# A grouped-query attention kernel: first K piece in two halves, early transposes moved behind score tiles, last period's order rewritten

## The chip, the cores and the metric

The kernel runs on one core of one Trainium2 chip. The metric is device time in microseconds (us), as a median of several executions; lower is better. The profile below is of one execution of the kernel before.

## The reference, cut to what matters

```python
batch, seq, n_heads, n_kv_heads, dim = 8, 512, 32, 8, 64      # float32 Q, K, V
K_expanded = np.repeat(K, 4, axis=2)                          # 4 heads of Q share one of K and V
V_expanded = np.repeat(V, 4, axis=2)
scores  = np.einsum('bhqd,bhkd->bhqk', Q, K_expanded) * scale # scale = 1/8, no mask
weights = np.exp(scores - scores.max(-1, keepdims=True))
weights = weights / (weights.sum(-1, keepdims=True) + 1e-10)
output  = np.einsum('bhqk,bhkd->bhqd', weights, V_expanded)
```

## The kernel before, in words

**Tiling.** Work is cut into 128 pairs of heads. For each pair the scores are made with the keys on the partitions, 128 keys at a time, so there are four score tiles of 128 x 1024 for a pair (512 queries of two heads side by side), and 512 in all. A score tile is two matmuls of 512 columns (line 241, in `scores`), which use the two halves of the array's rows beside each other. The exponential of a tile goes to ScalarE (ACT, line 255), or, for 78 of the 512 tiles, to a chain of steps on VectorE (DVE) and GpSimd (POOL) that builds the exponential out of bit patterns: `U` (line 266) and `F` (line 271) on DVE, `G` (line 276) and `W` (line 284) on POOL, and the join `P` (line 288) on DVE. The weighted sum with V (line 304, in `pv`) is 16 matmuls of 65 columns for each key chunk; the 65th column is the sum of the weights. `R` (line 320) takes the reciprocal of that sum and `N` (line 331) multiplies and writes the result; a store follows (line 372).

**Order.** The order of all this is written out by hand. `STEPS` (line 39) is the order of one period of 8 pairs, with 27 tiles on ACT and 5 on DVE and POOL, and 16 periods are run. `FINISH` (line 50) takes its place in the last one. A word of it is a step: `S9` fills the ninth score tile of ACT's list and `A9` is its exponential; `V1.6-8` is the last quarter of the weighted sum of pair 1; `D`, `U`, `F`, `G`, `W`, `P` with a number are the chain of that DVE tile; `T` and `C` transpose Q and copy it, `K` and `H` check V, `R` and `N` end a pair, `B` and `E` are small checks. `@1` names the period before, `a` and `b` the PSUM region. Each engine takes its own instructions strictly in that order: what stands behind a waiting instruction on TensorE (PE) waits too. There are two PSUM buffers for score tiles, so `S` of one tile waits until the exponential two tiles back is done.

**The opening.** Before the first period the kernel loads Q's first two heads (`q_start`, line 498) and K's first two heads (`k_start`, line 500) from the SP queue. K comes in two transfers: key chunk 0 (64 KB), then chunks 1 to 3 (192 KB). Further pieces come from the POOL queue (lines 505 to 516; `load_q` is line 149), with a few memsets in between. PE begins with eight idle matmuls of 512 columns on zeros (`spin`, line 493). DVE casts Q (line 522), ACT casts both K pieces (line 524), PE transposes Q (line 192 in `trans_q`) and K (line 171 in `first_k`), and DVE copies the transposes from PSUM (lines 195 and 173). PE's order is: spins, transposes of Q, transposes of K chunk 0, one more spin, transposes of K chunks 1 to 3, then score tiles. The transposes of what else the first two units need are listed in `EARLY` (line 214) by the number of the exponential behind which they are issued (line 437); all of them pass through the one buffer `d_ps`. Where the first period has no pair to sum yet, each `V` step of the order is replaced by as many idle matmuls of 256 columns as it has eighths (line 540).

The kernel ends with a flag: if a check fails, a general path runs instead (not run here).

Of the kernel before, what the change touches and what calls it, by code (L numbers as in the profile page):

```python
# [48 lines left out]
).split()  # L49
FINISH = (  # L50
# [10 lines left out]
).split()  # L61


# [19 lines left out]
def fast_path(ctx, tc, Q, K, V, out, flag):  # L83
    nc = tc.nc
    B, S, H, D = Q.shape
    KV = K.shape[2]
    HPG = H // KV
    SC = S // 128
# [38 lines left out]
    kn, qn, kt, qt = {}, {}, {}, {}  # L127

    def load_k(b, lo=0, hi=KV):
        if b not in kn:  # L130
            kn[b] = knat_pool.tile([128, SC, KV, D], BF16, name="k_nat")
        nc.gpsimd.dma_start(
            out=kn[b][:, :, lo:hi, :],
            in_=K[b, :, lo:hi, :].rearrange("(p sc) g d -> p sc g d", p=128),
        )
# [7 lines left out]
    def load_q(w, cuts=(0, 4 * HPG)):  # L143
        b, half = divmod(2 * w, GP)
        h0 = half * 2 * HPG
        if w not in qn:
            qn[w] = qnat_pool.tile([128, SC, 4 * HPG, D], BF16, name="q_nat")
        for lo, hi in zip(cuts[:-1], cuts[1:]):
            nc.gpsimd.dma_start(  # L149
                out=qn[w][:, :, lo:hi, :],  # L150
                in_=Q[b, :, h0 + lo:h0 + hi, :].rearrange("(sc p) h d -> p sc h d", p=128),
            )

    def d_tile():
        return d_pool.tile([128, 2, S], FP32, name="d_ps")
# [4 lines left out]
    def s_tile():  # L160
        return s_pool.tile([128, 2, S], FP32, name="s_ps")
# [4 lines left out]
    def first_k(gp, g, bank, lo=0, hi=SC):  # L166
        half_bank = bank.bitcast(BF16)[:, 0:S]
        ps = half_bank.rearrange("p (sc c) -> p sc c", sc=SC)
        for sc in range(lo, hi):
            for half in (0, 64):  # L170
                nc.tensor.transpose(ps[half:half + 64, sc, :], kn[0][:, sc, 2 * gp + g, :], ident)  # L171
        keys = slice(lo * 128, hi * 128)
        return lambda: nc.vector.tensor_copy(
            out=kt_first[:, gp, g, keys], in_=half_bank[:, keys]
        )
# [11 lines left out]
    def trans_q(u, g, bank, lo=0, hi=NPAIR):  # L187
        ps = bank.bitcast(BF16).rearrange("p (i sc c) -> p i sc c", i=NPAIR, sc=SC)
        for i in range(lo, hi):
            for sc in range(SC):  # L190
                h = ((u % 2) * 2 + g) * HPG + 2 * i
                nc.tensor.transpose(ps[:, i, sc, :], qn[u // 2][:, sc, h:h + 2, :], ident)  # L192
        if u not in qt:
            qt[u] = qt_pool.tile([128, 2, NPAIR, S], BF16, name="qt")
        return lambda: nc.vector.tensor_copy(  # L195
            out=qt[u][:, g, lo:hi, :], in_=ps[:, lo:hi, :, :].rearrange("p i sc c -> p i (sc c)")
        )
# [10 lines left out]
    def early_q(g, lo):  # L208
        return lambda bank: trans_q(0, g, bank, lo)

    def early_k(gp, g):
        return lambda bank: first_k(gp, g, bank)

    EARLY = {1: [early_q(0, 1)], 2: [early_k(0, 1)], 3: [early_q(1, 0)], 5: [early_k(1, 0)],
             6: [early_k(1, 1)]}

    every = [(p, kc) for p in range(PPAIR) for kc in range(SC)]
    ON_DVE = [(p, kc) for p, kc in every if kc in DVE_KCS[p]]
# [30 lines left out]
    def fill(p, kc):  # L249
        ps = s_tile()  # L250
        scores(p, kc, ps)
        filled[p, kc] = ps
# [166 lines left out]
    def step(tok, n):  # L419
        what, k = tok[0], int(tok[1:].split(".")[0].rstrip("ab"))  # L420
        q, kc = ON_DVE[k] if what in "DUFGWPgwsa" else (0, 0)
        if what == "S":
            fill(n * PPAIR + ON_ACT[k][0], ON_ACT[k][1])
            if k == 9 and n == 0:
                dma_k(0, TURNED)
            if k == 2 and n % 2 == 1 and n // 2 + 1 < B:
                dma_k(n // 2 + 1)
        elif what == "A":
            q, kc = ON_ACT[k]
            p = n * PPAIR + q  # L430
            exp_act(p, kc)
            if ON_ACT[k + 1:k + 2] == [] or ON_ACT[k + 1][0] != q:
                for d, (dq, dkc) in enumerate(ON_DVE):
                    if dq == q and not on_dve(n, d):
                        fill(p, dkc)
                        exp_act(p, dkc)
            if n == 0 and k in EARLY:
                bank = d_tile()
                for copy in [turn(bank[:, 1, :]) for turn in EARLY[k]]:
                    copy()  # L440
            if (n, k) == (0, 4):
                second_loads()
        elif what in "VRN":
            p = n * PPAIR + k
            if what == "V":
                lo, hi = tok[3:].rstrip("abs").split("-")
                pv(p, int(lo), int(hi), tok)
            else:
                (inverse if what == "R" else norm)(p)
        elif what in "TKCH":  # L450
            j = n * PPAIR // NPAIR + k
            if j < 2:
                pass
            elif what == "T":
                transposes(j, region(tok))
            elif what == "K":
                check_values(j)
            else:
                read(j if what == "C" else (j, "v"))
        elif what == "Q":  # L460
            loads(n, k)
        elif what == "B":
            if n < NPER - 1:
                bulk_check(n)
        elif what == "E":
            (early_check, verdict)[k]()
        elif what in "sa":
            (fill if what == "s" else exp_act)(n * PPAIR + q, kc)
        elif on_dve(n, k):
            p = n * PPAIR + q  # L470
            if what == "D":
                exp_fill(p, kc, region(tok))
                return
            st = chain.get((p, kc))
            if what == "U":
                exp_bits(st)
            elif what == "F":
                exp_low(st)
            elif what in "Gg":
                slope(nc.gpsimd if what == "G" else nc.vector, st["f"], st["g"])  # L480
            elif what in "Ww":
                bend(nc.gpsimd if what == "W" else nc.vector, st["f"], st["g"], st["w"])
            elif what == "P":
                exp_join(p, kc)
# [9 lines left out]
                bank[:, 1, 0:columns], warm[:, 0:128], warm[:, 0:columns], start=True, stop=True  # L494
            )

    START = ((0, 1), (1, SC))
    nc.sync.dma_start(out=q_start, in_=Q[0, :, 0:2, :].rearrange("(sc p) h d -> p sc h d", p=128))  # L498
    for raw, (lo, hi) in zip(k_start, START):
        nc.sync.dma_start(  # L500
            out=raw[:, lo:hi, :, :],
            in_=K[0, :, 0:2, :].rearrange("(p sc) g d -> p sc g d", p=128)[:, lo:hi, :, :],
        )
    make_identity(nc, ident)
    load_q(0, (2, 4, 8))
    nc.gpsimd.memset(ones, 1.0)
    nc.gpsimd.memset(off, 0)
    for j in range(2):
        for c in (0, VW - 1):
            nc.gpsimd.memset(vt[j][:, :, :, c:c + 1], 1.0)  # L510
    load_k(0, 2, 4)
    load_q(0, (8, 16))
    load_v(0, 0, 1)
# [6 lines left out]
    nc.scalar.activation(out=early, in_=warm[:, 0:1], func=EXP, scale=scale)  # L520
    spin(8, S)
    nc.vector.tensor_copy(out=qn[0][:, :, 0:2, :], in_=q_start)
    for raw, (lo, hi) in zip(k_start, START):
        nc.scalar.copy(out=kn[0][:, lo:hi, 0:2, :], in_=raw[:, lo:hi, :, :])  # L524
    copies = [trans_q(0, 0, s_tile()[:, 0, :], 0, 1), first_k(0, 0, d_tile()[:, 0, :], 0, 1)]
    for copy in copies:
        copy()
    spin(1, S)
    copy = first_k(0, 0, s_tile()[:, 0, :], 1, SC)
    copy()  # L530

    for period in range(-2, NPER):
        for entry in STEPS if period < NPER - 1 else FINISH:
            tok, _, late = entry.partition("@")
            n = period - int(late or 0)
            if 0 <= n < NPER:
                step(tok, n)
            elif period == 0 and n < 0 and tok[0] == "V":
                lo, hi = tok[3:].rstrip("abs").split("-")
                spin(int(hi) - int(lo), S // 2)  # L540


def general_path(tc, Q, K, V, out):
# [114 lines left out]
```

## Time and profile before

| | |
|---|---|
| median of 3 runs | 415.19 us (413.82 to 415.45) |
| the profiled execution | 415.06 us, of which the span of the profile is 413.2 us |
| ACT busy | 400.7 us (97% of the span) |
| PE busy | 380.7 us (92%) |
| DVE busy | 334.3 us (81%) |
| POOL busy | 276.6 us (67%) |

All times in the profile are counted from the start of the span; 1.9 us of the profiled execution lie outside it. A row of the timeline has the start, the duration from the first start to the last end, the engine, the line, the operation, what it writes and reads with sizes, and the count; in brackets stands how long the engine was idle before it and who ended that. On ACT and PE the instructions overlap: one exponential alone takes 1.02 to 1.06 us while the next one starts about 0.92 us after it.

### The profile page before, as it was taken

The page shows a single profiled execution, that of the slowest core. Times are in us where ns is not written, and L with a number is a line of the kernel's source. Part 1 is how long each engine was busy: PE and PEld are TensorE (multiplying, and loading weights), DVE is VectorE, ACT ScalarE, POOL GpSimd, SP SyncE. Part 2 cuts the span into 40 slices and gives each one's busy share as a digit, 9 for nine tenths or more (in the row PEclk, how much of TensorE's full clock was granted, in tenths as well). Part 3 has the DMA queues.
Part 4 walks back from the last instruction along what each step waited for, and adds up shares of the span by engine and source line. Part 5 has one row for each costly group of instructions (what it writes and reads, how often), then busy time and mean ns, then how long its engine had stood idle before and what let it go on. Part 6 is the DMA issues. An engine that isn't in the chain of part 4 may idle for free.

```text
span 413.2 us, 13322 instructions
## 1 busy us (share of the span) xinstructions
PE 380.7 (92%) x5825; PEld 242.1 (59%) x5825; DVE 334.3 (81%) x617; ACT 400.7 (97%) x438; POOL 276.6 (67%) x208
## 2 busy tenths in 40 slices
PE   8999989899998999989899998999989899998995
PEld 3556656566565655656565565656656565665553
DVE  2488897878889788897878889788797878889885
ACT  4999999999999999999999999999999999999994
POOL 8066776677766677676676766667776677766750
PEclk9999999999999999999999999999999999999998
DMA  9969788687769797589865979849788698652205
GB/s 148 197 123 191 190 157 200 156 165 175 158 169 179 129 215 176 138 192 238 170 122 136 181 168 216 202 105 172 194 158 198 165 167 173 158 161 103 103 37 174
DMA packets 65406, 67.74 MB, mean 164 GB/s; under 512 B 35264, under 2 KB 39872, under 8 KB 65344
## 3 DMA queue, kind: packets, MB, share of 16 engines
q0 software_dynamic: 28128, 24.91, 41.1%
q1 hardware_dynamic: 37216, 41.95, 34.4%
q8 instruction: 46, 0.75, 0.7%
q14 instruction: 16, 0.13, 0.1%
HBM read 50.33 MB, written 33.55 MB: 203 GB/s over the span
## 4 chain that ended last, share of the span: by engine, by line
ACT 76%; PE 20%; DMA 1%; DVE 1%; issue 1%; SPq 0%; ACTq 0%
ACT pt L255 76%; PE s_ps L241 9%; PE pv L304 5%; PE d_ps L304 3%; DMA k_start<-in_K_dram 1%; PE pv L493 1%; PE d_ps L192 1%; DVE pt L288 0%; PE d_ps L171 0%; ACTq L255 0%; DVE o_sb L331 0%; PE s_ps L171 0%; ACT k_nat L524 0%; SPq L500 0%; SPq L498 0%
## 5 line engine op out<-in xcount | busy, mean ns | idle before, releaser
L255 ACT ACTIVATE pt<-s_ps 128x1024 f16<-128x1024 f32 x434 | 398.4, 1283 | 2.8 <-PE s_ps L241 2.8
L304 PEld LDWEIGHTS <-pt 128*128 128x128 f16 x4096 | 142.4, 98 | 65.9 <-issue 55.0
L241 PE MATMUL s_ps<-qt,kt 64*128 64x512 bf16 x810 | 158.8, 383 | 23.1 <-ACT pt L255 20.0
L284 POOL TENSOR_TENSOR w<-g,f 128x1024 bf16<-128x1024 bf16 x77 | 164.1, 2132 | 6.4
L276 POOL TENSOR_SCALAR g<-f 128x1024 bf16<-128x1024 int16 x77 | 80.5, 1045 | 115.7 <-DVE f L271 115.7
L304 PE MATMUL pv<-v,pt 128*128 128x65 bf16 x2560 | 114.8, 195 | 0.2
L241 PEld LDWEIGHTS <-kt 64*128 64x128 bf16 x960 | 57.0, 93 | 65.2 <-issue 34.9
L266 DVE TENSOR_SCALAR u<-d_ps 128x1024 int16<-128x1024 f32 x48 | 58.6, 1221 | 19.8 <-PE d_ps L241 19.8
L304 PE MATMUL d_ps<-v,pt 128*128 128x65 bf16 x1536 | 66.6, 194 | 1.2 <-DVE pt L288 0.9
L331 DVE TENSOR_TENSOR o_sb<-pv,inv 128x512 f32<-128x512 f32 x80 | 55.3, 692 | 2.8
L288 DVE TENSOR_TENSOR pt<-u,w 128x1024 uint16<-128x1024 int16 x78 | 54.3, 698 | 2.1 <-POOL w L284 1.1
L192 PEld LDWEIGHTS <-q_nat 128*128 128x128 bf16 x512 | 29.4, 98 | 14.7 <-issue 10.9
L266 DVE TENSOR_SCALAR u<-pv 128x1024 int16<-128x1024 f32 x30 | 36.5, 1216 | 0.0
L195 DVE COPY qt<-d_ps 128x1024 bf16<-128x1024 bf16 (+1 forms) x48 | 32.7, 680 | 3.4 <-PE d_ps L192 3.4
L331 DVE TENSOR_TENSOR o_sb<-d_ps,inv 128x512 f32<-128x512 f32 x48 | 33.2, 691 | 1.6
L271 DVE TENSOR_SCALAR f<-u 128x1024 int16<-128x1024 int16 x78 | 32.7, 419 | 0.1
L192 PE MATMUL d_ps<-ident,q_nat 128*128 128x128 bf16 x380 | 29.8, 222 | 0.0
L320 DVE RECIPROCAL inv<-pv 128x8 f32<-128x8 f32 x80 | 16.5, 206 | 10.5 <-PE pv L304 7.5
L320 DVE RECIPROCAL inv<-d_ps 128x8 f32<-128x8 f32 x48 | 10.0, 208 | 15.6 <-PE d_ps L304 15.1
L241 PE MATMUL d_ps<-qt,kt 64*128 64x512 bf16 x90 | 17.5, 375 | 0.0
L204 DVE TENSOR_REDUCE okv<-d_ps 128x1 f32<-128x128 f32 x31 | 8.9, 287 | 9.3 <-PE d_ps L203 9.3
L149 POOL DMA_DIRECT2D q_nat<-in_Q_dram x18 | 14.7, 815 | 0.2 <-issue 0.2
(49 smaller groups left out, 116.6 us busy)
## 6 DMA issues: line engine op xcount, KB each, us to landing
out_dram<-o_sb SPq DMA_DIRECT2D x31, 1024.0 KB, 5.8
q_nat<-in_Q_dram POOLq DMA_DIRECT2D x15, 1024.0 KB, 9.1
k_nat<-in_K_dram POOLq DMA_DIRECT2D x7, 512.0 KB, 5.2
kt<-kt SPq DMA_DIRECT2D x14, 256.0 KB, 4.4
v<-in_V_dram POOLq DMA_DIRECT2D x7, 512.0 KB, 7.8
out_dram<-o_sb SPq DMA_DIRECT2D x4, 256.0 KB, 2.5
q_nat<-in_Q_dram POOLq DMA_DIRECT2D x1, 512.0 KB, 7.1
v<-in_V_dram POOLq DMA_DIRECT2D x4, 128.0 KB, 7.8
```

Of the source, the lines that this page charges most:

```text
L192: nc.tensor.transpose(ps[:, i, sc, :], qn[u // 2][:, sc, h:h + 2, :], ident)
L195: return lambda: nc.vector.tensor_copy(out=qt[u][:, g, lo:hi, :], in_=ps[:, lo:hi, :, :].rearrange("p i sc c -> p i (sc c)"))
L241: nc.tensor.matmul(ps[:, m, :], keys[64 * m:64 * m + 64, g if early else g ^ m, kc * 128:(kc + 1) * 128], qt[u][64 * m:64 * m + 64, g, i, ...
L255: nc.scalar.activation(out=pt_of(p)[:, kc, :, :], in_=filled.pop((p, kc)), func=EXP, scale=scale)
L266: nc.vector.tensor_scalar(out=st["u"], in0=st["ps"], scalar1=A_U, scalar2=B_U, op0=ALU.mult, op1=ALU.add)
L271: nc.vector.tensor_single_scalar(out=st["f"], in_=st["u"], scalar=1023, op=ALU.bitwise_and)
L276: engine.tensor_scalar(out=g, in0=f, scalar1=-EXP_F1, scalar2=EXP_K * 2.0 ** (24 * (engine is nc.gpsimd)), op0=ALU.add, op1=ALU.mult,)
L284: engine.tensor_tensor(out=w, in0=g, in1=f, op=ALU.mult)
L288: nc.vector.tensor_tensor(out=pt_of(p)[:, kc, :, :].bitcast(U16), in0=st["u"], in1=st["w"], op=ALU.add)
L304: nc.tensor.matmul(sums[p][:, m, qc, :], pt_of(p)[:, kc, m, qc * 128:(qc + 1) * 128], vt[b % 2][:, kc, gp, g * (D + 1):(g + 1) * (D + 1)], ...
L320: nc.vector.reciprocal(out=invs[n][:, k], in_=sums[p][:, :, :, s:s + 1])
L331: nc.vector.tensor_tensor(out=osb[u][:, :, h:h + 2, :].rearrange("p qc m d -> p m qc d"), in0=sums.pop(p)[:, :, :, o:o + D], in1=invs[p // ...
```

## The change

Four things, in the diff's order from the bottom up:

1. K's first piece is loaded in two halves of two key chunks each (128 KB and 128 KB). ACT casts the first half, DVE the second. PE transposes the first half, fills the first score tile, and then transposes the second half. The single spin between the pieces goes.
2. The early transposes are issued right behind the score tile `S` of their number instead of behind the exponential `A` of that number. One of them (the first of Q's second group) moves from number 3 to number 4, and number 0 is new: it is the second half of K.
3. On POOL the first two loads of Q's further heads are issued behind the memsets instead of ahead of them. The idle matmuls in the first period have 128 columns instead of 256.
4. `FINISH` is written anew: same steps, another order. The other 15 periods keep `STEPS`.

```diff
 FINISH = (
-    "F1 V5.1-2@1 C1 V5.2-3@1 G1 S1 V5.3-4@1 H1 V5.4-6@1 A0 S2 P4@1 V7.0-1a@1 V5.6-7@1 "
-    "V7.1-2@1 V5.7-8@1 V7.2-3@1 A1 W1 V7.3-4@1 R5@1 S3 N5@1 V7.4-6@1 A2 S4 V6.0-2b@1 "
-    "V7.6-8@1 A3 V6.2-3@1 R7@1 S5 F0 V6.3-5@1 N7@1 V6.5-6@1 G0 A4 S6 V6.6-8@1 D2a A5 R6@1 S7 "
-    "W0 N6@1 U2 A6 S8 T2b A7 S9 C2 V1.0-4a F2 A8 S10 P0 V0.0-2b V1.4-6 P1 A9 S11 V0.2-3 G2 "
-    "V0.3-4 V1.6-8 A10 S12 R1 V0.4-5 N1 V0.5-7 W2 V0.7-8 A11 S13 R0 D3a N0 A12 S14 U3 "
...
-    "V6.7-8 V7.1-2 A25 V7.2-3 R6 V7.3-5 N6 V7.5-6 A26 V7.6-8 R7 N7 E1 "
+    "F0 P4@1 S1 V5.1-3@1 H1 G0 V5.3-4@1 C1 A0 S2 V5.4-8@1 W0 A1 S3 R5@1 V7.0-1a@1 N5@1 "
+    "V7.1-4@1 A2 S4 V6.0-4b@1 A3 V7.4-5@1 F1 S5 P0 V6.4-7@1 A4 V6.7-8@1 S6 G1 R6@1 V7.5-6@1 "
+    "N6@1 V7.6-8@1 A5 S7 R7@1 T2b W1 N7@1 A6 S8 C2 D2a U2 A7 S9 V0.0-5b A8 S10 F2 V0.5-8 G2 "
+    "A9 S11 R0 V1.0-1a N0 V1.1-4 A10 W2 S12 D3b V1.4-6 A11 S13 A12 P1 A13 U3 V1.6-8 S14 R1 "
...
+    "R6 V7.2-4 N6 V7.4-6 B0@2 A26 V7.6-8 R7 N7 E1 "
 ).split()
...
-    EARLY = {1: [early_q(0, 1)], 2: [early_k(0, 1)], 3: [early_q(1, 0)], 5: [early_k(1, 0)],
-             6: [early_k(1, 1)]}
+    EARLY = {0: [early_k(0, 0, SC // 2)], 1: [early_q(0, 1)], 2: [early_k(0, 1)],
+             4: [early_q(1, 0)], 5: [early_k(1, 0)], 6: [early_k(1, 1)]}
...
         if what == "S":
             fill(n * PPAIR + ON_ACT[k][0], ON_ACT[k][1])
+            if n == 0 and k in EARLY:
+                bank = d_tile()
+                for copy in [turn(bank[:, 1, :]) for turn in EARLY[k]]:
+                    copy()
...
-            if n == 0 and k in EARLY:
-                bank = d_tile()
-                for copy in [turn(bank[:, 1, :]) for turn in EARLY[k]]:
-                    copy()
...
-    START = ((0, 1), (1, SC))
+    START = ((0, SC // 2), (SC // 2, SC))
...
     make_identity(nc, ident)
-    load_q(0, (2, 4, 8))
     nc.gpsimd.memset(ones, 1.0)
...
+    load_q(0, (2, 4, 8))
     load_k(0, 2, 4)
...
-    for raw, (lo, hi) in zip(k_start, START):
-        nc.scalar.copy(out=kn[0][:, lo:hi, 0:2, :], in_=raw[:, lo:hi, :, :])
-    copies = [trans_q(0, 0, s_tile()[:, 0, :], 0, 1), first_k(0, 0, d_tile()[:, 0, :], 0, 1)]
-    for copy in copies:
+    (lo, mid), (mid, hi) = START
+    nc.scalar.copy(out=kn[0][:, lo:mid, 0:2, :], in_=k_start[0][:, lo:mid, :, :])
+    for copy in [
+        trans_q(0, 0, s_tile()[:, 0, :], 0, 1), first_k(0, 0, d_tile()[:, 0, :], lo, mid)
+    ]:
         copy()
-    spin(1, S)
-    copy = first_k(0, 0, s_tile()[:, 0, :], 1, SC)
-    copy()
+    nc.vector.tensor_copy(out=kn[0][:, mid:hi, 0:2, :], in_=k_start[1][:, mid:hi, :, :])
...
-                spin(int(hi) - int(lo), S // 2)
+                spin(int(hi) - int(lo), S // 4)
```

More of the change, by code (lines that the diff above doesn't have):

```diff
@@ L209, in early_q, with early_k @@
         return lambda bank: trans_q(0, g, bank, lo)
-    def early_k(gp, g):
-        return lambda bank: first_k(gp, g, bank)
-    EARLY = {1: [early_q(0, 1)], 2: [early_k(0, 1)], 3: [early_q(1, 0)], 5: [early_k(1, 0)],
-             6: [early_k(1, 1)]}
+    def early_k(gp, g, lo=0):
+        return lambda bank: first_k(gp, g, bank, lo)
+    EARLY = {0: [early_k(0, 0, SC // 2)], 1: [early_q(0, 1)], 2: [early_k(0, 1)],
+             4: [early_q(1, 0)], 5: [early_k(1, 0)], 6: [early_k(1, 1)]}
     every = [(p, kc) for p in range(PPAIR) for kc in range(SC)]
```

8 rows, old and new, of the table FINISH are left out of this document.

## The prediction, as it was made

> **What bounds the kernel now.** I read the page first, then the chain of waits from end to end, then the timeline of the first 17 us and of the last 30.
>
> ```profile
> span 413.2 us, 13322 instructions
> PE 380.7 (92%) x5825; PEld 242.1 (59%) x5825; DVE 334.3 (81%) x617; ACT 400.7 (97%) x438; POOL 276.6 (67%) x208
> L255 ACT ACTIVATE pt<-s_ps 128x1024 f16<-128x1024 f32 x434 | 398.4, 1283 | 2.8 <-PE s_ps L241 2.8
> L276 POOL TENSOR_SCALAR g<-f 128x1024 bf16<-128x1024 int16 x77 | 80.5, 1045 | 115.7 <-DVE f L271 115.7
> L288 DVE TENSOR_TENSOR pt<-u,w 128x1024 uint16<-128x1024 int16 x78 | 54.3, 698 | 2.1 <-POOL w L284 1.1
> ```
>
> ScalarE is the bound: 434 exponentials fill 97% of the span and it is idle only 2.8 us among them. The change alters neither their number nor their size, so it can only move the first one, close gaps between them, or shorten what follows the last.
>
> ```profile
> 17.19 11.11 ACT pt L255 x12
> 78.28 6.86 ACT pt L255 x8
> 127.78 6.86 ACT pt L255 x8
> 391.03 2.05 DVE pt L288 x2
> 407.87 0.43 PE d_ps L304 x8
> 409.03 0.60 DVE o_sb L331
> ```
>
> The chain (start, length) repeats itself in the middle. The same place comes at 78.28 and two periods of 27 exponentials later at 127.78, so the steady pace is 49.50/54 = 0.917 us. That is the yardstick for both ends. The middle periods keep their order, and I cost them at nothing.
>
> **The opening now.** Its rows of the timeline:
>
> ```profile
> 3.73 0.30 ACT L524 CAST k_nat<-k_start 128x128 bf16<-128x128 f32 x1 [1.35 <-DMA k_start<-in_K_dram]
> 5.28 0.32 PE L171 MATMUL d_ps<-ident,k_nat 128*64 128x128 bf16 x2
> 5.39 0.42 DVE L195 COPY qt<-s_ps 128x512 bf16<-128x512 bf16 x1 [1.27 <-PE s_ps L192]
> 5.73 0.21 DVE L173 COPY kt_first<-d_ps 128x128 bf16<-128x128 bf16 x1
> 6.07 0.51 ACT L524 CAST k_nat<-k_start 128x384 bf16<-128x384 f32 x1 [2.04 <-DMA k_start<-in_K_dram]
> 6.63 0.53 PE L171 MATMUL s_ps<-ident,k_nat 128*64 128x128 bf16 x6 [0.49 <-ACT k_nat L524]
> 7.10 1.13 PE L241 MATMUL s_ps<-qt,kt_first 64*128 64x512 bf16 x4
> 7.21 0.36 DVE L173 COPY kt_first<-s_ps 128x384 bf16<-128x384 bf16 x1 [1.26 <-PE s_ps L171]
> 7.62 0.10 PEld L241 LDWEIGHTS <-kt_first 64*128 64x128 bf16 x2 [0.42 <-DVE kt_first L173]
> 7.75 1.94 ACT L255 ACTIVATE pt<-s_ps 128x1024 f16<-128x1024 f32 x2 [1.17 <-PE s_ps L241]
> 8.16 0.61 PE L493 MATMUL pv<-warm 128*128 128x256 bf16 x2
> 8.56 0.64 PE L192 MATMUL d_ps<-ident,q_nat 128*128 128x128 bf16 x4
> 8.99 0.64 PE L493 MATMUL pv<-warm 128*128 128x256 bf16 x2
> 9.56 0.61 PE L241 MATMUL s_ps<-qt,kt_first 64*128 64x512 bf16 x2
> 10.21 2.87 ACT L255 ACTIVATE pt<-s_ps 128x1024 f16<-128x1024 f32 x3 [0.52 <-PE s_ps L241]
> 10.64 0.39 PE L241 MATMUL s_ps<-qt,kt_first 64*128 64x512 bf16 x2
> 12.18 0.61 PE L192 MATMUL d_ps<-ident,q_nat 128*128 128x128 bf16 x8
> 12.83 0.69 DVE L195 COPY qt<-d_ps 128x1024 bf16<-128x1024 bf16 x1 [0.99 <-PE d_ps L192]
> ```
>
> Both operands of the first score tile are in SBUF at 5.94 (5.73 + 0.21). It starts at 7.10 because PE is in order and stands at 6.63 waiting for the large K piece. From 7.75 to 17.19 nine exponentials start; at 0.917 they would take 8.25, so 1.19 us are lost on top of the late start. PE is slow here: a tile takes 0.61 at 9.56 and 0.39 at 10.64. Until about 10.6 a tile holds PE for 0.54 before the idle matmuls that follow (7.62 to 8.16), a transpose of 128 columns for 0.107 (four from 8.56 to 8.99), and a change of matmul shape costs about 0.11 (included in the 0.54).
>
> **The change there, step by step.** *First tile.* K's first 64 KB were in at 3.73 and all 256 KB at 6.05; in proportion to bytes the new 128 KB half lands at 4.50. Its cast of 256 columns lies between 0.30 and 0.51; I take 0.40, so 4.90, which is before PE is through with Q at 5.28. Its four transposes (between the 0.32 of two and the 0.53 of six) take 0.42. The copy to SBUF starts at 5.73 as now and takes 0.28 (between 0.21 and 0.36): 6.02. The tile starts 0.05 later, as at 7.62, needs 0.61, and ACT begins 0.04 after its end: 6.07 + 0.61 + 0.04 = 6.72, **1.03 before** 7.75.
>
> *Second half.* It lands by 6.05, the same bytes in all. DVE is free then and casts it in about 0.33 (ACT's rows give 0.30 to 0.51): 6.38. PE reaches its transposes at 6.07 + 0.54 = 6.61 and the second tile at 6.97; that tile ends at 7.58, and the second exponential is due at 6.72 + 0.92 = 7.64. The new wait is covered, by 0.06 only: a half that comes 0.5 later costs about 0.3.
>
> *Tiles 3 and 4.* Behind tile 2 now stand four Q transposes and then four spins at 0.107: 6.97 + 0.54 + 0.43 + 0.43 + 0.13 for the change of shape = 8.50, done 9.11, exponential at 9.15; due 7.64 + 0.92 = 8.56, lost 0.59. Behind it eight K transposes side by side in twos (0.43), two spins (0.21) and two changes of shape: 8.50 + 0.54 + 0.43 + 0.21 + 0.22 = 9.90, exponential at 10.55; due 10.07, lost 0.48. Tile 5 starts at 9.90 + 0.54 + 0.21 + 0.11 = 10.76, now fast, and is in time.
>
> *Later.* The eight Q transposes go from behind exponential 3 to behind tile 4. At about 12.6 their 0.69 copy starts, and the K transposes behind the next tile wait for the one buffer; the tile queued behind those comes about 0.24 late. Losses are 0.59 + 0.48 + 0.24 = 1.31 against 1.19 now. **The opening gives 1.03 - 0.12 = 0.91 us.** From the rows it may be 0.2 (halves 0.5 to 1 us later than by bytes) to 1.9 (PE fast from 8.5, so that 0.59 and 0.48 go).
>
> *POOL.* Two loads go behind the memsets:
>
> ```profile
> 1.61 1.71 POOL L149 DMA_DIRECT2D q_nat<-in_Q_dram  x2 [0.16 <-issue]
> 3.31 0.12 POOL L506 MEMSET ones<- 128x1 bf16 x1
> 3.43 0.40 POOL L510 MEMSET v<- 128x16 bf16 x4
> q_nat<-in_Q_dram POOLq DMA_DIRECT2D x1, 128.0 KB, 4.7
> ```
>
> The memsets take about 0.5 (3.31 to 3.83), so this piece lands at 1.61 + 0.5 + 4.7 = 6.8 instead of 6.3. PE wants it at 6.97 + 0.54 = 7.51: hidden, by 0.7. The loads behind keep their places. K's halves share the DMA engines with it for half a microsecond less, which is worth nothing to a few tenths; I take nothing.
>
> **The last period.**
>
> ```profile
> 379.05 14.08 ACT L255 ACTIVATE pt<-s_ps 128x1024 f16<-128x1024 f32 x15
> 390.95 2.13 DVE L288 TENSOR_TENSOR pt<-u,w 128x1024 uint16<-128x1024 int16 x2
> 391.12 1.41 POOL L276 TENSOR_SCALAR g<-f 128x1024 bf16<-128x1024 int16 x1 [1.30 <-DVE f L271]
> 393.13 0.41 PE L304 MATMUL d_ps<-v,pt 128*128 128x65 bf16 x8 [0.87 <-DVE pt L288]
> 393.91 13.91 ACT L255 ACTIVATE pt<-s_ps 128x1024 f16<-128x1024 f32 x15 [0.78 <-PE s_ps L241]
> ```
>
> Fifteen starts lie between 379.05 and 393.91: 14.86 us, 1.11 more than 15 x 0.917. The last fifteen run at pace (14 x 0.917 + 1.06 = 13.90). The stall is one place: `P0 P1` stand together on DVE beside POOL's G2, all three slow (2.13 for two instead of 2 x 0.70, 1.41 instead of 1.05), `V1.6-8` waits for P1, and `S12` is queued behind it.
>
> In the new order P0 comes after `F1`, five score tiles before `V0.5-8`. P1 follows `N0`: after pair 0's sum come R0, N0 and P1, some 0.2 + 0.7 + 0.7 us, while three score tiles (2.75) are placed between `V0.5-8` and `V1.6-8`, whose matmuls and those of V1 fill PE. So P1 has about half a microsecond in hand beyond what PE needs; the 0.37 that a join grew by here fits in. The rest of the order spreads the joins in the same way. I take 1.0 of the 1.11 back; nothing if a new pile-up is as bad, and up to 1.5 if the small gaps of the steady pace go too.
>
> *Tail.* After the last exponential come the same eight matmuls (407.87), the same DVE steps to 409.63 and the same store; `B0@2` moves ahead of it, where DVE waits anyway. Nothing, within 0.2.
>
> **Sum:** 0.91 + 1.0 = 1.9, made against the profiled execution's 415.06: **413.1**. That execution stands 0.1 below the median of 415.19.
>
> **Rivals.**
>
> *PE is fast sooner, or the last period runs smoother than the middle.* Without the 0.59 and 0.48 the opening gives 1.0 more: 412.0. For it: PE idles less after 6.1 than now. Against it: nothing in the trace sets the moment.
>
> *PE is fast later.* The idle matmuls that kept it busy are halved, and one of 512 columns goes. If it stays slow to about 14, the eight Q transposes (0.86) with three spins and the tile make a slot of 1.8 instead of 0.92; with the slot before, 0.16 + 0.91 - 0.24 = 0.83 is lost: 413.9.
>
> *Slower than before: PE stays slow far into the weighted sums.* From 17 on a slot needs a tile (0.54) and 16 matmuls of 65 columns at 0.054 (half the 0.107): 1.41 instead of 0.92, a loss of 0.35 per us. The gain of 1.9 is gone at 14 + (1.9 - 0.83)/0.35 = 17, and at 24 the kernel stands at 417.4. Against it: once these sums begin PE has no gap left. The Trainium skill, "TensorE: Matmul & The Clock Gate", says in Part 1 that the clock is released by a busy window of some 3.4 us at a phase that the kernel doesn't set, and in Part 4 that transposes don't count as busy. By that rule the two last rivals gain, since in the new opening transposes take the place of idle matmuls between 7.5 and 10.6; the fast row at 10.64 after four transposes in the stretch neither confirms nor excludes it.
>
> *It doesn't do what it says.* The last period stalls again at another join, or a K half lands a microsecond late: one of the two gains falls away, 414.1.
>
> **How the numbers follow.** About 0.5% (2.1 us) is what a measurement of this kernel can tell from no change. Forecast 0.62, with its own range 412.4 to 413.8, a little more than half of it beyond the bound: 0.34 faster, 0.28 same. PE sooner or a smoother end 0.14, faster. PE later 0.08, same. One gain missing 0.08, same. Slower 0.08. Together 0.48, 0.44, 0.08. The range 411.8 to 414.8 leaves out the slow rival and the ends of the others.
>
> **What would show it.** The first exponential starts at about 6.7 and the second without a gap; PE transposes K's second half between the first two tiles. The tenth exponential starts about 0.9 before 17.19. No exponential of the last period waits 0.5 us for PE, and no join is waited for by PE. The prediction is wrong if tiles still take 0.61 after 11 us, if DVE's cast of the second half ends after 6.6, or if the middle periods change their pace.

## The result, and the profile after

The changed kernel takes 411.90 us (median of 6 runs, 411.44 to 412.04). The kernel before took 414.98 beside it (6 runs, 413.82 to 415.45). The ratio is 0.993, with a 95% interval of 0.9915 to 0.9945: faster by 3.1 us, where the forecast was 1.9 (413.1, with a range of 411.8 to 414.8).

The profiled execution took 411.91 us, 3.15 less than the one profiled before. Its page:

```profile
span 410.1 us, 13319 instructions
PE 377.7 (92%) x5824; PEld 242.2 (59%) x5824; DVE 334.1 (81%) x618; ACT 399.9 (98%) x437; POOL 276.6 (67%) x208
L254 ACT ACTIVATE pt<-s_ps 128x1024 f16<-128x1024 f32 x434 | 398.0, 1292 | 2.2 <-PE s_ps L240 2.2
```

The lines have moved up by one (254 was 255, 240 was 241, 303 was 304). The same 434 exponentials are there, and ScalarE's wait for score tiles is 2.2 us in place of 2.8; all 2.2 now lie ahead of the first exponential. The timeline of the opening of the changed kernel:

```profile
4.03 0.40 ACT L523 CAST k_nat<-k_start 128x256 bf16<-128x256 f32 x1 [1.65 <-DMA k_start<-in_K_dram]
4.72 0.63 PE L191 MATMUL s_ps<-ident,q_nat 128*128 128x128 bf16 x4
5.29 0.42 PE L170 MATMUL d_ps<-ident,k_nat 128*64 128x128 bf16 x4
...
6.10 0.45 PE L240 MATMUL s_ps<-qt,kt_first 64*128 64x512 bf16 x2 [0.40 <-DVE kt_first L172]
6.49 0.30 PE L170 MATMUL d_ps<-ident,k_nat 128*64 128x128 bf16 x4
6.60 13.98 ACT L254 ACTIVATE pt<-s_ps 128x1024 f16<-128x1024 f32 x15 [2.16 <-PE s_ps L240]
6.72 0.39 PE L240 MATMUL s_ps<-qt,kt_first 64*128 64x512 bf16 x2
...
8.64 0.39 PE L240 MATMUL s_ps<-qt,kt_first 64*128 64x512 bf16 x2
```

PE fills the first tile (6.10), transposes K's second half (6.49) and fills the second tile (6.72), as laid out. The exponentials run from 6.60 on as one row of 15. And a score tile takes 0.39 from the second one on; before, a tile still took 0.61 at 9.56. PE has its full clock some 4 us sooner (6.27 instead of 10.67). No term of the forecast's sum had that; one of its rivals did.

The last period of the changed kernel, and the end of its chain of waits:

```profile
373.11 31.55 ACT L254 ACTIVATE pt<-s_ps 128x1024 f16<-128x1024 f32 x34
379.71 0.68 DVE L287 TENSOR_TENSOR pt<-u,w 128x1024 uint16<-128x1024 int16 x1
...
390.10 0.75 DVE L287 TENSOR_TENSOR pt<-u,w 128x1024 uint16<-128x1024 int16 x1
```

```profile
404.72 0.43 PE pv L303 x8
...
405.88 0.60 DVE o_sb L330
```

Thirty-four exponentials in a row, with no idle time before any; the last one alone is 1.24 long, so the 33 starts before it took 30.31, against 33 x 0.917 = 30.26. The joins shown (0.68 and 0.75) stand alone, where two took 2.13 before, and the other four of this stretch take 0.68 or 0.69.

**Where the 3.15 came from**, by the starts of the exponentials in the two traces:

| | before | after | gain |
|---|---|---|---|
| first exponential | 7.75 | 6.60 | 1.15 |
| from there to the tenth | 9.44 (at 17.19) | 8.37 (at 14.97) | 1.07 |
| to the last but one ahead of the last period's `A0` | 362.77 | 362.68 | 0.09 |
| the 28 starts after that one | 26.81 | 25.77 | 1.04 |
| from the last start to the end of the span | 6.45 | 6.64 | -0.19 |

The last 28 starts are the one ahead of `A0` and the 27 of the last period. Counted from `A0` itself, its 26 further starts take 25.00 before and 23.89 after: 1.11, and the middle gives 0.01.

### The profile page after: what moved, and what is told of

Same layout as the page of the kernel before. It is cut to its first block, busy times and chain, and to the rows that moved or that the text cites. A ratio compares the mean times of both kernels' runs of the same rounds, so it can differ in the third digit from the quotient of the medians.

```text
span 410.1 us, 13319 instructions
## 1 busy us (share of the span) xinstructions
PE 377.7 (92%) x5824; PEld 242.2 (59%) x5824; DVE 334.1 (81%) x618; ACT 399.9 (98%) x437; POOL 276.6 (67%) x208
## 4 chain that ended last, share of the span: by engine, by line
ACT 77%; PE 20%; issue 1%; DVE 1%; ACTq 0%
ACT pt L254 77%; PE s_ps L240 9%; PE pv L303 6%; PE d_ps L303 4%; PE pv L492 1%; PE d_ps L191 0%; DVE qt L194 0%; ACTq L254 0%; DVE o_sb L330 0%; PE s_ps L191 0%; PE d_ps L170 0%; PE d_ps L202 0%; DVE warm L517 0%; DVE kt_first L172 0%; DVE off L343 0%
## 5 line engine op out<-in xcount | busy, mean ns | idle before, releaser
L265 DVE TENSOR_SCALAR u<-d_ps 128x1024 int16<-128x1024 f32 x47 | 57.4, 1221 | 19.9 <-PE d_ps L240 19.9
L287 DVE TENSOR_TENSOR pt<-u,w 128x1024 uint16<-128x1024 int16 x78 | 53.4, 685 | 2.2 <-POOL w L283 0.8
L265 DVE TENSOR_SCALAR u<-pv 128x1024 int16<-128x1024 f32 x31 | 37.7, 1216 | 0.0
```

The lines of the kernel that those rows point to most:

```text
L265: nc.vector.tensor_scalar(out=st["u"], in0=st["ps"], scalar1=A_U, scalar2=B_U, op0=ALU.mult, op1=ALU.add)
L287: nc.vector.tensor_tensor(out=pt_of(p)[:, kc, :, :].bitcast(U16), in0=st["u"], in1=st["w"], op=ALU.add)
```

## The experiments

**The theories.** Two things were to be told apart. *The order theory:* the opening gains by its order alone (halves, tiles that start sooner, fewer idle matmuls), and PE's full clock at 6 in one profile was chance. *The clock theory:* a good part of the opening's gain is PE's clock; the new order leaves PE no long idle stretch at 6 us, and so the clock opens sooner in most executions. For the last period, the theory was that P1's lateness behind P0 makes the stall, and the rival that the stall is spread over the whole old order. The kernels were measured in three groups, each with its own runs of the kernel before (21, 17 and 10 of them); each ratio is to those.

**1. The opening alone** (`e1_open`): the changed kernel with the old order of the last period.

```diff
 FINISH = (
-    "F0 P4@1 S1 V5.1-3@1 H1 G0 V5.3-4@1 C1 A0 S2 V5.4-8@1 W0 A1 S3 R5@1 V7.0-1a@1 N5@1 "
...
+    "F1 V5.1-2@1 C1 V5.2-3@1 G1 S1 V5.3-4@1 H1 V5.4-6@1 A0 S2 P4@1 V7.0-1a@1 V5.6-7@1 "
...
```

> The changed kernel with the last period's order of before: only the opening is changed. If the opening brings the 0.91 us of the prediction and about 1.1 more because its own work makes PE fast sooner (tiles of 0.39 from the second on), the time is 2.0 to 2.2 us under before, near 412.8, in every run. If the early fast PE was a chance of the executions measured, the runs spread as those of before do (1.6 us), with a median about 0.9 under before, near 414.0.

Measured: 412.86 (10 runs, nine of them 412.62 to 413.09, one 414.24), ratio 0.9957 (0.994 to 0.9974). The stall of the last period is there again; in the timeline of this kernel:

```profile
388.64 2.12 DVE L288 TENSOR_TENSOR pt<-u,w 128x1024 uint16<-128x1024 int16 x2
...
391.60 13.91 ACT L255 ACTIVATE pt<-s_ps 128x1024 f16<-128x1024 f32 x15 [0.78 <-PE s_ps L241]
```

So the opening is worth about 2.1 (414.93 to 412.86), more than twice the forecast's 0.91, and it takes nothing from the last period. The ten runs lie close together but for one, while the 21 runs of the kernel before beside them fall into two groups: ten from 413.6 to 414.4, eleven from 414.9 to 416.5.

**2. The last period alone** (`e2_finish`): the kernel before with the new `FINISH` (the diff above the other way round).

> Before with the last period's new order alone. If the stall of 1.11 us at 393.91 goes as predicted, the time is about 1.0 us under before, near 414.0, and the first exponential stays at 7.75. If the last period's gain only shows together with the new opening, or a new join stalls, it is within 0.3 us of before.

Measured: 414.23 (12 runs, 412.75 to 415.76), ratio 0.9981 (0.9964 to 0.9998). By its trace the last 28 starts take 25.68 instead of 26.81, a gain of 1.13; the medians show 0.70, within the interval's 0.1 to 1.5. The runs spread as those of the kernel before do, since the old opening is in it. Together the two parts give 2.07 + 0.70 = 2.8 of the 3.1.

Its profile caught PE's clock going back. In the busy times by stretch (stretch and its length, PE busy, matmuls, granted clock, DMA share, GB/s) of this kernel:

```profile
0.93:4.34 3.41, 3.01 (x8) 1.00 0.54 136
4.34:7.76 3.42, 1.77 (x17) 1.00 1.41 166
7.76:11.17 3.41, 3.36 (x16) 0.50 1.31 185
```

The granted clock in the trace is full at 4.34, half at 7.76 and full again at 11.17: steps of 3.41. (Ahead of the first record of a trace the column shows 1.00 whatever the clock is; there the length of a tile tells it, 0.61 or 0.39.) Between 4.34 and 7.76 PE was idle for 1.57 in one stretch, in wait for the large K piece.

**3. The kernel before, once more** (`e3_before_again`), unchanged, to see whether the moment of the full clock is a property of that kernel.

> The kernel before once more, for one question: at what moment the tiles go from 0.61 to 0.39 us. If the kernel's own work sets it, again between 10.3 and 10.7. If the phase is free, anywhere from about 6 to 11, and the losses of the opening follow: near 0.5 us if fast by 8, 1.2 if at 10.6.

Measured: 413.96, one run, in the lower of the two groups. Its opening:

```profile
6.83 0.36 PE L171 MATMUL s_ps<-ident,k_nat 128*64 128x128 bf16 x6 [0.95 <-ACT k_nat L524]
7.12 0.92 PE L241 MATMUL s_ps<-qt,kt_first 64*128 64x512 bf16 x4
7.55 13.23 ACT L255 ACTIVATE pt<-s_ps 128x1024 f16<-128x1024 f32 x14 [0.78 <-PE s_ps L241]
8.74 0.39 PE L241 MATMUL s_ps<-qt,kt_first 64*128 64x512 bf16 x2
```

Here the old order has PE at full clock (from 5.38) and no exponential after the first is late by 0.2 or more. The tenth one starts at 16.09 instead of 17.19. The same kernel, 1.1 us apart, with the clock's moment as the one difference seen that could gain it (K's second piece was cast 0.20 later here, at 6.27): the moment isn't fixed. It also gives the order's worth at a full clock: 16.09 to 14.97, 1.12, good to a few tenths, since K lands at different times in the two.

**4. Idle matmuls of 256 columns again** (`e5_spin256`), in the changed kernel.

```diff
-                spin(int(hi) - int(lo), S // 4)
+                spin(int(hi) - int(lo), S // 2)
```

> The changed kernel with idle matmuls of 256 columns in the first period, as before. If PE is fast early anyway, the wider ones cost 0.1 us a slot in places: one or two tiles come 0.1 to 0.3 late, and the time is 412.0 to 412.3. If the halved width is what keeps the opening in time, as with a slow PE, 0.43 is added in each of two slots: 412.8.

Measured: 412.16 (4 runs, 411.98 to 412.24), ratio 0.9931 (0.9904 to 0.9958). That is 0.26 above the changed kernel's 411.90, which was not measured beside it; in the traces the tenth exponential starts 8.51 after the first instead of 8.37. By the traces the shorter idle matmuls are worth a tenth or two, and they are not what opens the clock (5.65 here).

**5. The halves alone** (`e6_halves`): the kernel before with K's two halves and the first tile between them, with the old places of the other early transposes, the old idle matmuls, POOL's old order and the old last period.

```diff
...
+            if n == 0 and k == 0:
+                early_k(0, 0, SC // 2)(d_tile()[:, 1, :])()
...
-    START = ((0, 1), (1, SC))
+    START = ((0, SC // 2), (SC // 2, SC))
...
-    for raw, (lo, hi) in zip(k_start, START):
-        nc.scalar.copy(out=kn[0][:, lo:hi, 0:2, :], in_=raw[:, lo:hi, :, :])
...
+    nc.scalar.copy(out=kn[0][:, lo:mid, 0:2, :], in_=k_start[0][:, lo:mid, :, :])
...
-    spin(1, S)
...
+    nc.vector.tensor_copy(out=kn[0][:, mid:hi, 0:2, :], in_=k_start[1][:, mid:hi, :, :])
```

> Before with one part of the opening alone: K in two halves, the first tile between them, and no spin there; the early transposes stay behind the exponentials, the idle matmuls have 256 columns, POOL's order and the last period are those of before. If the opening's gain is the wait for K that goes from PE's queue, the first exponential is at 6.5 to 6.8 and the time close to that of the whole new opening, 412.9 to 413.3, with few runs above. If the moved transposes, the narrower idle matmuls or POOL's order carry it, it stays at 413.9 to 415.

Measured: 413.39 (6 runs: 413.25 to 413.50 and one 414.94), ratio 0.9948 (0.9936 to 0.996). The profile is of the run of 414.94; it has PE slow until 10.60:

```profile
6.75 2.12 ACT L255 ACTIVATE pt<-s_ps 128x1024 f16<-128x1024 f32 x2 [2.20 <-PE s_ps L241]
9.78 3.05 ACT L255 ACTIVATE pt<-s_ps 128x1024 f16<-128x1024 f32 x3 [0.91 <-PE s_ps L241]
13.12 7.58 ACT L255 ACTIVATE pt<-s_ps 128x1024 f16<-128x1024 f32 x8 [0.29 <-PE s_ps L241]
```

At a slow clock, of the first exponential's lead of 1.00 only 0.43 is left at the third (9.78 against 10.21; it waits 0.91, where the old one waits 0.52), and the tenth starts at 16.93, only 0.26 before 17.19. The other five runs are 1.5 faster; an earlier full clock would do that, but none of them was profiled. By its ratio the halves alone gain as much (415.64 to 413.39, 2.25) as the whole new opening in experiment 1 (2.07): the moved transposes, the narrower idle matmuls and POOL's order add nothing that these runs can show.

**6. One token** (`e7_p1`): as experiment 1, with P1 moved ahead in the old last period.

```diff
-    "W0 N6@1 U2 A6 S8 T2b A7 S9 C2 V1.0-4a F2 A8 S10 P0 V0.0-2b V1.4-6 P1 A9 S11 V0.2-3 G2 "
+    "W0 N6@1 U2 A6 S8 T2b A7 S9 P1 C2 V1.0-4a F2 A8 S10 P0 V0.0-2b V1.4-6 A9 S11 V0.2-3 G2 "
```

> The new opening with the last period's old order, in which one step alone is moved: P1 from behind V1.4-6 to behind S9, ahead of the copy C2. If the stall of the last period is the join P1 that comes late on DVE, it goes: the 30 last exponentials run at the steady pace and the time is 411.8 to 412.0, all that the new last period gives. If the old order stalls at other joins too, half or more of the 1.0 stays: 412.4 or more.

Measured: 411.82, 412.36, 413.30 and 413.41; ratio 0.9936 (0.9916 to 0.9955). The runs are too far apart for the times to decide, but the trace does:

```profile
373.26 31.72 ACT L255 ACTIVATE pt<-s_ps 128x1024 f16<-128x1024 f32 x34
387.48 0.81 DVE L288 TENSOR_TENSOR pt<-u,w 128x1024 uint16<-128x1024 int16 x1
389.34 0.68 DVE L288 TENSOR_TENSOR pt<-u,w 128x1024 uint16<-128x1024 int16 x1
```

The joins stand alone and no exponential waits idle. The last 28 starts take 26.13, where the old order took 26.90 (experiment 1) and the new one 25.77: one token gives 0.77 of the 1.13, and the largest loss left is 0.27, at 390.16. P1 behind P0 was most of the stall; the other 0.36 was elsewhere in the old order.

**7. The old opening with the wait filled** (`e8_fill`): the kernel before with three idle matmuls of 512 columns between the K pieces instead of one.

```diff
-    spin(1, S)
+    spin(3, S)
```

> Before with three idle matmuls of 512 columns in place of one between the K pieces, so that PE is busy while it would wait for K. If that idle stretch is what lets the clock stay or fall to half in a part of the executions, the runs near 415.2 go and nearly all lie near 414.0 (413.8 to 414.4). If the phase alone decides, the two groups stay, with a median of 414.5 to 415.

Measured: 414.61 (12 runs, eleven of them 414.13 to 414.95, one 415.86), ratio 0.998 (0.9968 to 0.9992). The opening, in the busy times by stretch and in the timeline of this kernel:

```profile
3.84:7.25 3.41, 3.15 (x12) 1.00 1.29 171
```

```profile
7.33 0.36 PE L171 MATMUL s_ps<-ident,k_nat 128*64 128x128 bf16 x6 [0.34 <-ACT k_nat L524]
8.05 12.31 ACT L255 ACTIVATE pt<-s_ps 128x1024 f16<-128x1024 f32 x13 [0.77 <-PE s_ps L241]
9.24 0.39 PE L241 MATMUL s_ps<-qt,kt_first 64*128 64x512 bf16 x2
```

With the idle stretch filled the clock opens at 7.25 in this profile, and eleven of the twelve runs lie within 0.82 us (the 17 runs of the kernel before beside them go from 413.82 to 416.66). The first exponential is 0.30 later, as its K piece came late (cast at 6.77), and the tenth still starts 0.60 sooner than 17.19. The spread is as the first branch of the expectation has it, but the median is not: 414.61 instead of 414.0 lies in the range of the second. Why it is that much higher isn't shown; the idle matmuls themselves hold PE to 6.99 (5.53 + 1.46), past the 6.63 at which the kernel before began K's transposes. For the clock theory it is the plainest case: nothing but busy time was added.

**8. Half the idle matmuls ahead** (`e9_lead4`): the changed kernel with four of 512 columns at the start instead of eight.

```diff
-    spin(8, S)
+    spin(4, S)
```

> The changed kernel with four instead of eight idle matmuls ahead, so that PE is fast later. If the rest of the forecast's working holds for a slow PE, the losses at tiles 3 and 4 come (0.59 and 0.48) and the time is about 1.1 over that of the changed kernel, 412.9 to 413.2, more if the clock opens after 11. If the new opening does not depend on the clock, it stays at 411.9 to 412.1.

Measured: 413.41 (4 runs, 413.36 to 413.82), ratio 0.9952 (0.9937 to 0.9967): its four runs lie 1.5 to 1.9 above the changed kernel's median. Its busy times by stretch and its timeline:

```profile
0.42:3.83 3.41, 1.89 (x4) 1.00 0.46 132
3.84:7.25 3.41, 1.96 (x16) 1.00 1.13 137
7.25:10.66 3.41, 3.41 (x26) 1.00 1.22 164
```

```profile
6.50 1.02 ACT L254 ACTIVATE pt<-s_ps 128x1024 f16<-128x1024 f32 x1 [1.85 <-PE s_ps L240]
6.51 0.29 DVE L528 CAST k_nat<-k_start 128x256 bf16<-128x256 f32 x1 [0.72 <-DMA k_start<-in_K_dram]
7.87 1.02 ACT L254 ACTIVATE pt<-s_ps 128x1024 f16<-128x1024 f32 x1 [0.34 <-PE s_ps L240]
...
9.37 1.02 ACT L254 ACTIVATE pt<-s_ps 128x1024 f16<-128x1024 f32 x1 [0.48 <-PE s_ps L240]
10.16 0.61 PE L240 MATMUL s_ps<-qt,kt_first 64*128 64x512 bf16 x2
10.81 9.40 ACT L254 ACTIVATE pt<-s_ps 128x1024 f16<-128x1024 f32 x10 [0.42 <-PE s_ps L240]
```

This is the new opening with PE slow until 10.66, the case that the forecast had worked out. Between the starts 7.87, 9.37 and 10.81 lie 1.50 and 1.44: tile 3 loses 0.58 and tile 4 loses 0.52, where the forecast had 0.59 and 0.48. (Tile 2 loses 0.45 as well, because K's second half was cast only at 6.51.) The tenth exponential starts at 16.44. The order's worth at a slow clock is then 17.19 - 16.44 = 0.75, with tile 2's loss in it.

**9. The changed kernel, once more** (`e10_after_again`), unchanged.

> The changed kernel once more. If its opening keeps PE busy enough to be fast early whatever the phase, the runs stay together at 411.4 to 412.2. If the phase still decides in a part of them, as in before, a second group stands about 1.1 higher, near 413.0 to 413.4, and its share says how much of the 3.1 us of the first result was the clock.

Measured: 411.93 (6 runs: four of 411.79 to 411.99, then 413.13 and 413.35), ratio 0.9929 (0.991 to 0.9948) to 415.37. The profile has the full clock from 5.35 and the tenth exponential at 15.05. Of the twelve runs of this kernel ten lie from 411.44 to 412.04; the two at 413.1 to 413.4 are near experiment 8, but were not profiled.

**10. A further step** (`e11_lead7_q3`): the changed kernel with seven idle matmuls at the start and Q's second group back behind tile 3.

```diff
-             4: [early_q(1, 0)], 5: [early_k(1, 0)], 6: [early_k(1, 1)]}
+             3: [early_q(1, 0)], 5: [early_k(1, 0)], 6: [early_k(1, 1)]}
...
-    spin(8, S)
+    spin(7, S)
```

> The changed kernel with seven idle matmuls ahead instead of eight, and the eight Q transposes of the second group behind tile 3 instead of tile 4. Q is cast at 4.0 to 4.1 while the eighth idle matmul holds PE to 4.7, so the first exponential can start up to 0.4 earlier if K's half is in time, and the tile that is 0.21 late at 13.1 is in time: 411.3 to 411.6 if the clock still opens early. If the eighth idle matmul is what fills the window of the clock, a part of the runs is 1.1 slower.

Measured: 412.24 (6 runs, 411.34 to 414.14), ratio 0.9933 (0.991 to 0.9956). The first exponential starts at 6.04 in its profile, but the second then waits for K's second half (0.16), and the runs spread over 2.8 us; three of the six lie 0.7 to 2.2 above the changed kernel's 411.90, much as the second case of the expectation has it, though none of these was profiled. Two things were changed at once, so neither is told apart. It isn't shown to be better than the changed kernel; no version here is.

**11. POOL's loads ahead of the memsets again** (`e12_pool`), in the changed kernel.

```diff
+    load_q(0, (2, 4, 8))
     nc.gpsimd.memset(ones, 1.0)
...
-    load_q(0, (2, 4, 8))
```

> The changed kernel with POOL's two loads ahead of the memsets, as before. By the prediction nothing to a few tenths: both K halves land within 0.3 us of 4.03 and 5.96, the times of the changed kernel, and the first exponential starts at 6.6 (6.75 with a slow PE). If the order on POOL is what lets the halves land early, the second half lands at 6.3 or later and the second exponential is late by 0.3.

Measured: 411.73, one run; first exponential at 6.41, tenth at 14.78, 8.37 apart as in the changed kernel. K's first half was cast at 4.73, later than the expected 0.3 around 4.03 (3.98 to 4.63 in the kernels with the new order on POOL and eight idle matmuls ahead); it cost nothing, as PE came to it at 5.19. The second half was in time (cast at 5.84). POOL's order makes no difference that one run can show.

**12. The early transposes alone** (`e13_early`): the kernel before, with the list issued behind `S` and number 3 moved to 4.

```diff
-    EARLY = {1: [early_q(0, 1)], 2: [early_k(0, 1)], 3: [early_q(1, 0)], 5: [early_k(1, 0)],
+    EARLY = {1: [early_q(0, 1)], 2: [early_k(0, 1)], 4: [early_q(1, 0)], 5: [early_k(1, 0)],
...
             fill(n * PPAIR + ON_ACT[k][0], ON_ACT[k][1])
+            if n == 0 and k in EARLY:
+                bank = d_tile()
+                for copy in [turn(bank[:, 1, :]) for turn in EARLY[k]]:
+                    copy()
...
-            if n == 0 and k in EARLY:
-                bank = d_tile()
-                for copy in [turn(bank[:, 1, :]) for turn in EARLY[k]]:
-                    copy()
```

> Before with the early transposes behind the tiles, alone. The first exponential stays at 7.55 to 7.75. With a fast PE the losses up to the tenth exponential stay 0.2 to 0.4; with a slow PE the third tile is late by less than now (0.64), since two idle matmuls no longer stand ahead of its transposes' copy, by 0.1 to 0.2. It is worth at most 0.3.

Measured: 416.73, one run. K's second piece came late (cast at 6.87) and PE was slow until 13.65, so that the first exponential starts at 8.55 and the tenth at 18.86; what the edit is worth in all stays open. What was expected of the third tile at a slow clock did not come: it is as late as in the kernel before (1.54 from the second start to the third in both), not 0.1 to 0.2 less. The run also shows a late clock: this is the prediction's rival of a PE that is slow to about 14, in the old opening.

**The openings side by side**, from the traces (PE at full speed from; first and tenth exponential):

| kernel | opening | full speed | first | tenth |
|---|---|---|---|---|
| before | old | 10.67 | 7.75 | 17.19 |
| `e3_before_again` | old | 5.38 | 7.55 | 16.09 |
| `e2_finish` | old | 4.34 to 7.76, then 11.17 | 7.72 | 17.52 |
| `e13_early` | old, early moved | 13.65 | 8.55 | 18.86 |
| `e8_fill` | old, wait filled | 7.25 | 8.05 | 16.59 |
| `e6_halves` | halves only | 10.60 | 6.75 | 16.93 |
| after | new | 6.27 | 6.60 | 14.97 |
| `e1_open` | new | 5.34 | 6.50 | 14.87 |
| `e7_p1` | new | 6.70 | 6.75 | 15.12 |
| `e10_after_again` | new | 5.35 | 6.50 | 15.05 |
| `e12_pool` | new | 5.03 | 6.41 | 14.78 |
| `e5_spin256` | new, 256 columns | 5.65 | 6.53 | 15.04 |
| `e11_lead7_q3` | new, 7 ahead | 4.36 | 6.04 | 14.58 |
| `e9_lead4` | new, 4 ahead | 10.66 | 6.50 | 16.44 |

Both theories hold a half. With eight or seven idle matmuls ahead the new opening has PE fast by 6.7 in all seven profiles; the old one (with its wait and the early transposes at their old places) in one of three for good. Between the two profiled kernels the tenth exponential moves by 2.22: 1.10 is the clock (17.19 to 16.09 in the same old order) and 1.12 the order at a full clock (16.09 to 14.97), each good to a few tenths, as K's landing moves too.

Every run, profiled or not, has its mean granted clock on record, and this bears it out. In the profiles the mean is 0.996 or more, but for `e2_finish`, whose clock went back: 0.993 (3.41 us at half speed take 0.004 off the mean of such a span). Of the 48 runs of the kernel before beside the experiments, 24 have 0.991 to 0.994, and each of these took 415.1 or more; of the other 24, 17 took less than 414.8. With the wait filled (`e8_fill`) one run of twelve has such a clock (0.992, at 415.86), in `e1_open` one of ten (0.993, at 414.24), and in the changed kernel none of twelve. By this sign the old opening lost the clock again in half of its runs, and its wait for K is what loses it. The changed kernel's two late runs (0.999 and 0.998) did not lose it; a late first opening would fit them, but isn't shown.

## Why the prediction was right or wrong, step by step

**The sign and the places were right.** The gain came in the opening and in the last period, and the middle gave 0.09 or less. The number was met by a narrow margin, and not by the sum: 411.90 lies 1.2 under the forecast's 413.1, outside its own 412.4 to 413.8, and 0.1 above the lower end of the whole range, which reached so far down for a rival.

*First tile.* Forecast 6.72, measured 6.60, and 6.41 to 6.75 in the other kernels with this opening and eight idle matmuls ahead. K's first half was cast at 3.98 to 4.73; 4.50 was the estimate of its landing. Where PE was still slow for the first tile (`e7_p1`) it is 6.75, as worked out; in the changed kernel that tile took 0.45 instead of 0.61, which makes up the 0.12.

*Second half.* It was transposed between the tiles and the second exponential came without a gap. The forecast's thin cover of 0.06 was right in kind: `e10_after_again` cast it at 6.49 and its second exponential came 0.10 late; with PE slow (`e9_lead4`, cast at 6.51) it came 0.45 late, where the forecast had about 0.3 for half a microsecond. In `e10_after_again` the cast ends at 6.78, past the 6.6 that the forecast named as a sign of being wrong; in the changed kernel's own profile none of its signs appears.

*Tiles 3 and 4.* **This step failed.** "Lost 0.59" and "lost 0.48" rested on "until about 10.6 a tile holds PE for 0.54": the clock's moment was read off one profile and taken as a property of the kernel. At that clock the sum is right (0.58 and 0.52 in `e9_lead4`), but in most executions of the new opening PE is fast before tile 3, and nothing is lost there. The rival "PE is fast sooner" was the case that came, at its 412.0, with a chance of 0.14. What spoke against it, "nothing in the trace sets the moment", was true of that one trace; the moment is set by how busy PE is in each stretch of 3.41 us and by where these stretches fall, and the change alters the first of the two. For the whole opening the forecast had 0.91, the traces have 2.22.

*Later.* Forecast 0.24 late behind the large copy; the eighth exponential (13.14) came 0.21 late. The rows of the changed kernel's chain of waits:

```profile
6.60 3.78 ACT pt L254 x4
...
11.40 0.69 DVE qt L194
...
13.14 13.46 ACT pt L254 x15
```

*POOL.* Forecast nothing; `e12_pool` shows nothing. The terms were off, though: the memsets put the loads back by 0.16 (1.61 to 1.77), not by 0.5, and the margin ahead of PE is not the 0.7 of the forecast (6.8 to 7.51), as both ends move. The piece landed 4.2 after its issue in the changed kernel, at about 6.0, and 5.2 after it in `e7_p1`, at about 7.0; PE, fast by then, loads it at 7.04 and 7.20. The two rows, of the changed kernel and of `e7_p1`:

```profile
7.04 0.34 PEld L191 LDWEIGHTS <-q_nat 128*128 128x128 bf16 x4 [0.23 <-issue]
```

```profile
7.20 0.35 PEld L192 LDWEIGHTS <-q_nat 128*128 128x128 bf16 x4 [0.23 <-DMA q_nat<-in_Q_dram]
```

The idle 0.23 is the same in both, so the second row's DMA isn't shown to hold PE; but in `e7_p1` only some 0.2 were left.

*The last period.* Forecast 1.0 of 1.11, measured 1.04 (1.11 from `A0` on); no exponential waited for P1. That the pile-up of P0 and P1 is the stall, `e7_p1` shows for 0.77 of 1.13.

*Tail.* Forecast nothing within 0.2, measured -0.19: the last exponential was 1.24 long instead of 1.06. It is 1.24 in `e2_finish` too, and 1.06 in the profiles with the old last period, so it comes with the new order; why isn't shown.

*The slower rival* (PE slow far into the sums) and *PE is fast later* didn't come in any profile of the new opening as it stands; `e9_lead4` shows 10.66 as the late case. The two gains did not fail either.

## What to carry to other kernels

Where an engine's clock depends on its recent work, an edit near the start is judged by the busy time that it leaves in each stretch, not only by the work on the path; take several profiles of the kernel before, and read a spread of its times in two groups as a sign that the moment isn't fixed. Work out the sum once for each clock, and give the chances by how busy the engine will be. A stall in an order written by hand can be mostly one token, as here (0.77 of 1.13): move that one alone first, and see how much of the gain it holds.

## What the runs showed of the hardware

**The clock's moment is a question of PE's busy time in stretches of 3.41 us.** Beside those of `e2_finish`, `e8_fill` and `e9_lead4` above stand the busy times by stretch of the kernel before,

```profile
0.44:3.85 3.41, 2.52 (x6) 1.00 0.43 117
3.85:7.26 3.41, 2.92 (x18) 1.00 1.32 164
7.26:10.67 3.41, 3.41 (x18) 1.00 1.32 186
```

of the changed kernel (up to its full clock),

```profile
2.86:6.27 3.41, 3.01 (x15) 1.00 1.18 186
```

and of `e7_p1`:

```profile
3.29:6.70 3.41, 3.02 (x16) 1.00 1.18 166
```

Each stretch is counted back from the moment of the full clock in steps of 3.41, the distance that `e2_finish` shows. Of the stretches shown, PE went to full speed behind those with 3.01 and more, and not behind those with 2.92 and less. That is close together, but the view counts a modelled end each time that PE stops: four transposes at 0.107 (0.43) stand as 0.63 at 4.72. Without such ends (0.17 each, an estimate from all matmul rows of the fourteen profiles) the clock opened behind every stretch with 2.65 or more of 3.41 and behind none with 2.51 or less. In the profiles it fell back once within the kernel's work, behind the 1.77 of `e2_finish` (1.08 without the ends), and stayed with 1.29 (`e11_lead7_q3`, 4.36 to 7.77). A stretch that is partly idle is enough to lose it.

The Trainium skill, "TensorE: Matmul & The Clock Gate", Part 1, has a free-running window of this length; the 3.41 between the records of `e2_finish` agrees, and so does the free phase: the full clock comes anywhere from 4.36 to 6.70 in the seven profiles of nearly the same opening.

**Transposes count as busy here.** Of the 3.02 of `e7_p1` idle matmuls are 1.64 and the first score tile 0.60. These 2.24 alone would not have opened the clock, since the 2.52 of idle matmuls alone in the first stretch of the kernel before didn't; the rest of the 3.02 is transposes. The Trainium skill, "TensorE: Matmul & The Clock Gate", Part 4, states that a transpose doesn't count in the same way; the measurement differs from it, and the forecast's sentence that by this rule the two late rivals gain falls with it.
